# A Hymba-style block on one core: squares of x on two engines, parameter rows through GpSimd's queue, low parts of w_in on VectorE, scan parameters in steps

## The chip, the cores and the metric

One core of a Trainium2 chip runs the whole kernel. The metric is the device time of one execution in microseconds (us). The engines are named as in the profile: PE is TensorE, DVE VectorE, ACT ScalarE, POOL GpSimd, SP SyncE; each has an instruction queue of its own and takes its instructions in order.

## The reference

The input x has 1024 tokens of 1024 features, c is one conditioning vector. Cut to what matters here:

```python
c_act = jax.nn.silu(c)
mod = c_act @ ada_w + ada_b                  # shift, scale, gate, twice
h = modulate(rms_norm(x, norm1_g), sh1, sc1)
proj = h @ w_in                              # 1024 x (256 u, 3 x 512 q k v, 8 f, 3 x 256 conv)
u, q, k, v, f_logit, hc, bg, cg = split(proj)
y_ssm  = s5_mixer(u, ...)                    # complex scan over time, 16 groups of 64 states
y_attn = fox_attention(q, k, v, f_logit)     # rms_norm of q and k per head, forget gate, 8 heads of 64
y_conv = bg * conv3(cg * hc)
y = rms_norm(concat(y_ssm, y_attn, y_conv) per head) @ w_out
x = x + g1 * y
x = x + g2 * moe(modulate(rms_norm(x, norm2_g), sh2, sc2))   # 16 experts, top 2
```

In s5_mixer every state has `ab = exp(lam * dt)` (a magnitude `mag`, a sine and a cosine of `li * dt`); the kernel needs its first eight powers, the factor `z` of b, and the eighth power's phase.

## The kernel before

Matmuls of f32 data are done as three products of high and low parts: for a weight chunk in `feed` (L253) the high part is a copy by ACT into a rounded type (L280) and the low part a subtraction (`tt`, L95, called at L281). w_in comes in 40 chunks of 128x2x256; the first 8 low parts are on DVE, the 32 others on POOL. A projection group is 24 matmuls: high x high, low x high, high x low.

The order on every engine is the order in which the code is written. Four stretches concern the change.

**Start.** `load_x` (L156) issues x0 to x3 in turn from SP's and ACT's queues, SP then the ada_w blocks (`load_ada`, L308, the transfer at L314) and w_in chunks. ACT's queue further issues c_in (L202) and the five parameter rows into `prow` (L205, L207), then `Silu` of c (L216) and the four squares of the first half's tokens with their sums (`x_sq`, L432). The DMAs of SP and ACT share eight completion lanes, so a ninth waits until the first has landed. On PE `pvp` (L471) turns `prow`; DVE copies its parts out (L472 to L477), then makes the reciprocal root (`x_rs`, a chain from L123 over L110 to L115), scales x (L442), and PE turns it (`x_turn`, L447).

**The two loops over b (L536 and L972).** For half 0 and then half 1 of the tokens, each step turns x, makes h and its low part (`x_mod`: ACT L460, DVE L463 and L95) and multiplies with the conv channel hc (`groups`, L501). `sincos` (L370) and `s5_small` (L574), some 90 small DVE instructions on 128x8 to 128x32 elements that make the scan's parameters, stand behind the second loop.

**Conv and u groups.** `conv_group` for cg and bg and `u_group` (L951) are interleaved by `step`, one yield at a time, with generators: `s5_prep` (L622: products `ta`, `tb` with the powers on DVE, turns `pt` at L680, the kernel matrices `gk` by matmuls `pg` at L693 and L695), `s5_turns` (L707, complex powers on POOL in `tr` and `vroom`), and `conv_norm` (`pn`, L927). The result u goes to DRAM (`ud`) and comes back in another layout.

**q, k and v.** `project_steps` (L1026) makes a 128-token tile of q or k, ACT copies it (L1138) and squares it head by head (L1143), DVE copies the forget logits out (`f_sb`, L1140). `qk_norm` (L1040) puts the norm, the split and the turns into `later`, each for a beat counted in projections: QC, QD for q and KC, KD_ for k. `s5_main` (L779) is stepped between: once per projection until UG of them are done, twice after; its first yields lead to `px` (L796, the input of the scan, out of `ud`), then the two scans (L805, L807), `vv`, and `py` (L832).

Of the kernel before, what the change touches and what calls it, by code (L numbers as in the profile page):

```python
# [81 lines left out]
def _emit(tc, nc, V, A, G, T, I, out, dump, upto, stack):  # L82
# [386 lines left out]
    V.tensor_copy(cst[:, :, 0], c_act)  # L469
    pvp = ps_ms.tile([P, P], F32, name="pvp", tag="ms")  # L470
    T.transpose(pvp, prow, identF)  # L471
    V.tensor_copy(pv, pvp[:, :NPV])  # L472
    V.tensor_copy(lr, pvp[:, NPV:NPV + 8])
    V.tensor_copy(li, pvp[:, NPV + 8:NPV + 16])
    V.tensor_copy(dsk, pvp[0:16, NPV + 16:NPV + 32])
    for two in range(2):
        V.tensor_copy(ldt[64 * two:64 * two + 64, :], ldt16[64 * two:64 * two + 64, two:16:2])  # L477

# [1797 lines left out]
```

## Time and profile before

| what | us |
|---|---|
| median of 3 runs (lowest, highest) | 1109.03 (1107.26, 1115.13) |
| profiled execution | 1109.11 |
| its span, first to last instruction | 1107.4 |
| PE busy | 1008.4 (91%) |
| DVE busy | 719.8 (65%) |
| ACT busy | 523.5 (47%) |
| POOL busy | 291.9 (26%) |

The profile belongs to one execution. 1.7 us of its time lie around the span. The mean clock granted to TensorE over the span is 0.954 of full. A matmul's busy time is modelled, so the table's share says how rarely PE stands, not how well it is used. Times of rows count from the span's start.

### The profile page before, as it was taken

What the parts mean: (1) busy time and instruction counts of PE and PEld (TensorE: products, weight loads), DVE (VectorE), ACT (ScalarE), POOL (GpSimd) and SP (SyncE); (2) the same over time, 40 slices, a digit from 0 to 9 for tenths busy, and PEclk for the clock granted to TensorE, in tenths of its full rate; (3) what the DMA queues carried; (4) which work ended last, traced back from release to release, by engine and by line L of the source; (5) the groups of instructions that cost most, each with busy time, mean ns of one, the idle gap of its engine ahead of it and who ended that gap; (6) DMA issues with size and microseconds to landing.
All of it is one profiled execution on the core that took longest, in us unless ns stands there. A gap on an engine that the chain in (4) does not pass through costs nothing. (4 is left out here: it accounts for less than half of the span.)

```text
span 1107.4 us, 17980 instructions
## 1 busy us (share of the span) xinstructions
PE 1008.4 (91%) x6273; PEld 825.1 (75%) x6273; DVE 719.8 (65%) x1576; ACT 523.5 (47%) x1099; POOL 291.9 (26%) x312
## 2 busy tenths in 40 slices
PE   2999798899989998998899994999999999999995
PEld 1677578788778987887788883677777777777773
DVE  3679512926723344778466778895657899789593
ACT  3541113346444554777532222764435676567470
POOL 3006913233312002118312234112222212122121
PEclk9999789899989999999899995899999999999998
DMA  9701135015875444466255634896788699979772
GB/s 304 270 1 39 39 73 121 20 59 177 264 268 173 124 130 137 117 190 199 69 152 185 245 133 133 312 353 227 223 266 285 239 366 360 378 238 355 259 264 41
DMA packets 103006, 215.63 MB, mean 195 GB/s; under 512 B 14094, under 2 KB 37148, under 8 KB 102748
## 3 DMA queue, kind: packets, MB, share of 16 engines
q1 hardware_dynamic: 89744, 170.93, 46.0%
q0 software_dynamic: 12032, 40.60, 13.2%
q10 hardware_dynamic: 1116, 2.67, 0.7%
q8 instruction: 61, 1.00, 0.4%
q14 instruction: 53, 0.43, 0.1%
HBM read 185.47 MB, written 28.10 MB: 193 GB/s over the span
## 5 line engine op out<-in xcount | busy, mean ns | idle before, releaser
L95 DVE TENSOR_TENSOR wel<-wer,weh 128x1024 fp32r<-128x1024 f32 x192 | 223.1, 1216 | 2.9 <-ACT weh L1929 1.3
L1929 ACT ACTIVATE weh<-wer 128x1024 fp32r<-128x1024 f32 x192 | 188.9, 1053 | 5.0 <-ACTq L2185 1.7
L1984 POOL DMA_INDIRECT out_dram<-y,idx x28 | 56.9, 2033 | 234.2 <-DVE y L2049 139.4
L2012 PE MATMUL pg<-weh,xh 128*128 128x512 f32 x256 | 104.7, 409 | 2.0 <-ACT hid L2170 0.7
L2013 PE MATMUL pg<-weh,xl 128*128 128x512 f32 x256 | 103.1, 403 | 0.0
L95 DVE TENSOR_TENSOR pl<-ptp,ph 128x512 fp32r<-128x512 f32 (+1 forms) x80 | 50.3, 636 | 40.0 <-ACT ph L1321 39.7
L2017 PE MATMUL pg<-wel,xh 128*128 128x512 f32 x256 | 66.3, 397 | 0.0
L2012 PEld LDWEIGHTS pg<-weh,xh 128*128 128x128 f32 x256 | 49.1, 192 | 17.9 <-issue 6.1
L1321 ACT ACTIVATE ph<-ptp 128x512 fp32r<-128x512 f32 (+1 forms) x80 | 44.1, 553 | 31.3 <-PE ptp L1316 30.5
L2013 PEld LDWEIGHTS pg<-weh,xl 128*128 128x128 f32 x256 | 49.1, 192 | 11.6 <-DVE xl L95 0.4
L2017 PEld LDWEIGHTS pg<-wel,xh 128*128 128x128 f32 x256 | 47.7, 188 | 11.3
L1303 ACT ACTIVATE lg<-lg,mn 128x128 f32<-128x128 f32 (+3 forms) x64 | 49.5, 774 | 10.6 <-DVE mn L1292 10.6
L1316 PE MATMUL ptp<-identF,lg 128*128 128x128 f32 x288 | 48.1, 285 | 6.5 <-DVE pl L95 6.3
L2039 PE MATMUL pd<-weh,hh 128*128 128x512 f32 x128 | 52.2, 408 | 0.6 <-ACT hh L2031 0.5
L293 PE MATMUL pmw<-woh,yh 128*128 128x512 f32 x128 | 52.6, 411 | 0.0
L295 PE MATMUL pmw<-woh,yl 128*128 128x512 f32 x128 | 51.1, 399 | 0.0
L2040 PE MATMUL pd<-wel,hh 128*128 128x512 f32 x128 | 50.5, 395 | 0.0
L1336 PE MATMUL po<-ph,vs 128*128 128x256 f32 (+1 forms) x160 | 47.1, 315 | 1.2 <-ACT ot L1340 1.0
L1998 ACT ACTIVATE xh<-ptx 128x512 fp32r<-128x512 f32 x32 | 19.1, 598 | 60.9 <-issue 57.7
L1968 POOL DMA_INDIRECT xg<-h2d,idx x16 | 21.0, 1314 | 89.7 <-DVE wgt L1955 86.3
L1138 ACT ACTIVATE r<-pm 128x256 f32<-128x256 f32 x32 | 12.3, 384 | 61.7 <-PE pm L298 54.6
L1337 PE MATMUL po<-pl,vs 128*128 128x256 f32 (+1 forms) x160 | 40.3, 286 | 0.2
(658 smaller groups left out, 2679.1 us busy)
## 6 DMA issues: line engine op xcount, KB each, us to landing
wer<-in_w_up_dram SPq DMA_DIRECT2D x64, 512.0 KB, 8.6
wer<-in_w_gate_dram SPq DMA_DIRECT2D x63, 512.0 KB, 9.4
wer<-in_w_down_dram SPq DMA_DIRECT2D x63, 512.0 KB, 10.5
adw<-in_ada_w_dram SPq DMA_DIRECT2D x32, 512.0 KB, 4.9
vroom<-in_ada_w_dram SPq DMA_DIRECT2D x16, 512.0 KB, 8.7
xt<-in_x_dram SPq DMA_DIRECT2D x14, 512.0 KB, 7.1
qtd<-qe POOLq DMA_DIRECT2D x16, 256.0 KB, 4.2
qt<-qtd SPq DMA_DIRECT2D x16, 256.0 KB, 5.3
```

The costliest lines, as they stand in the source:

```text
L95: (eng or V).tensor_tensor(o, a, b, op=op)
L293: T.matmul(o, lhsT=sh(k), rhs=mh(k), start=(k == 0), stop=False)
L295: T.matmul(o, lhsT=sl(k), rhs=mh(k), start=False, stop=False)
L1303: A.activation(lg[:, :w], lg[:, :w], AF.Exp, bias=mn, scale=-1.0, accum_out=l_all[:, qb, h:h + 1])
L1316: T.transpose(pt[:, c0:c0 + P], lgs[u, b][0][:, k0:k0 + P], identF)
L1929: A.activation(hi, raw, AF.Copy)
L1984: G.indirect_dma_start(out=out[:, :], out_offset=bass.IndirectOffsetOnAxis(ap=ix, axis=0), in_=y, in_offset=None, compute_op=ALU.add)
L2012: T.matmul(pg, lhsT=x[0][:, k, :], rhs=hi, start=(k == 0), stop=False)
L2013: T.matmul(pg, lhsT=x[1][:, k, :], rhs=hi, start=False, stop=False)
L2017: T.matmul(pg, lhsT=x[0][:, k, :], rhs=lo, start=False, stop=(k == KD - 1))
L2039: T.matmul(pd, lhsT=h[0][:, k, :], rhs=hi[:, n, :], start=(k == 0), stop=False)
L2040: T.matmul(pd, lhsT=h[0][:, k, :], rhs=lo[:, n, :], start=False, stop=False)
```

## The change

Eight edits. (1) c_in's transfer comes first on ACT's queue and `Silu` right behind the x loads; the five parameter rows go to POOL's queue. (2) `load_bc`'s six transfers of ssm_b and ssm_c go from POOL's queue to SP's. (3) The squares of x1 and x3 are made by DVE in one instruction that multiplies and sums; ACT keeps x0 and x2. (4) `pvp` and the copies out of it stand behind the turns of half 0 instead of ahead of its norm. (5) All low parts of w_in are on DVE. (6) `sincos` and `s5_small` are one generator, of which steps are taken within the two loops over b. (7) Two yields more ahead of `gk` in `s5_prep`; UG 4 to 6, QD 5 to 6, KD_ 3 to 4. (8) q's factor is multiplied by DVE instead of POOL, and `f_sb` is copied by ACT instead of DVE.

```diff
-QC, QD, KC, KD_ = 3, 5, 2, 3
+QC, QD, KC, KD_ = 3, 6, 2, 4
-UG = 4
+UG = 6
...
+    c_in = cp.tile([P, 8], F32, name="c_in")
+    nc.scalar.dma_start(out=c_in, in_=I["c"].rearrange("o (p t) -> (o p) t", t=8))
     for i in range(4):
         load_x(i, nc.scalar if i % 2 else nc.sync)
+    c_act = cp.tile([P, 8], F32, name="c_act")
+    A.activation(c_act, c_in, AF.Silu)
...
-        nc.scalar.dma_start(out=prow[r0:r0 + n, :], in_=I[nm].rearrange("(r c) -> r c", c=P))
+        nc.gpsimd.dma_start(out=prow[r0:r0 + n, :], in_=I[nm].rearrange("(r c) -> r c", c=P))
...
-            tt(lo, raw[:, :, :m_], hi.bitcast(F32), ALU.subtract, V if at_w[1] <= 8 else G)
+            tt(lo, raw[:, :, :m_], hi.bitcast(F32), ALU.subtract)
...
-    def sincos(x):
+    def sincos(x, out):
...
+        yield
         cq = small()
...
         V.tensor_scalar(cq, cq, 1.0, None, op0=ALU.add)
+        yield
...
         V.tensor_scalar(pos, m, 1.0, None, op0=ALU.is_equal)
+        yield
...
         for j in js:
-            sq = st.tile([P, D], BF16, name="sqx", tag="sqx", bufs=1)
-            A.activation(sq, xts[half * 4 + j], AF.Square, accum_out=ss[:, j:j + 1])
+            x_ = xts[half * 4 + j]
+            if half == 0 and j % 2:
+                sq = st.tile([P, D], BF16, name="sqv", tag="sqv", bufs=1)
+                V.tensor_tensor_reduce(out=sq, in0=x_, in1=x_, scale=1.0, scalar=0.0, op0=ALU.mult, op1=ALU.add,
+                                       accum_out=ss[:, j:j + 1])
+            else:
...
             mag = vexp(mul(lr, dt_))
+            params = s5_small()
+        if b > 1:
+            next(params)
...
+        yield
+        yield
         gk = s5b.tile([16, 16, 8, 16], F32, name="gk", tag="wv")
...
                 x_mod(1, k)
+        for _ in range(2 if b < 4 else 1):
+            next(params, None)
         if b:
             groups(b - 1, "hc", 1)
-    th = mul(li, dt_)
-    sn, cs = sincos(th)
+    for _ in params:
+        pass
     es_st.close()
-    s5_small()
...
-                tt(r32, r32, gq[:, None, :].to_broadcast([P, 16, HD]), ALU.mult, G)
+                tt(r32, r32, gq[:, None, :].to_broadcast([P, 16, HD]), ALU.mult)
...
-                        V.tensor_copy(X["f_sb"][:, :, i4 * 4 + i], pm[:, 256:264])
+                        A.activation(X["f_sb"][:, :, i4 * 4 + i], pm[:, 256:264], AF.Copy)
```

`s5_small` has a yield behind each of its three rounds of powers, behind `z`, and behind each of the three squarings of the phase; its arithmetic is the same.

On ACT at the start, before, from the c_in transfer to the last square (`prow` are the parameter rows, `xt` x, `sqx` the squares; DMAHW0 to 7 are the completion lanes):

```order
L202 DMA c_in_109<-in_c_dram 128x8
L205 DMA prow_80<-in_ada_b_dram 48x128 [waits DVE_49]
L205 DMA prow_80<-in_norm1_g_dram 8x128 [waits DMAHW0_49]
L205 DMA prow_80<-in_norm2_g_dram 8x128 [waits DMAHW1_49]
L205 DMA prow_80<-in_out_norm_g_dram 8x128 [waits DMAHW3_49]
L207 DMA prow_80<-in_conv_w_dram 6x128 [waits DMAHW4_49]
L216 ACT_TABLE_LOAD
L216 ACTIVATE c_act_121<-c_in_109 128x8 [waits DMAHW5_49]
L432 ACTIVATE sqx_187,ssx_186<-xt_72 128x1024
L432 ACTIVATE sqx_189,ssx_186<-xt_74 128x1024 [waits Activation_49]
L432 ACTIVATE sqx_191,ssx_186<-xt_76 128x1024 [waits DMAHW2_49,Activation_49]
L432 ACTIVATE sqx_193,ssx_186<-xt_78 128x1024 [waits Activation_49]
```

and of the change, from the first instruction to the first low-part work:

```order
L162 DMA c_in_72<-in_c_dram 128x8
L158 DMA xt_76<-in_x_dram 128x1024
L158 DMA xt_80<-in_x_dram 128x1024
L166 ACT_TABLE_LOAD
L166 ACTIVATE c_act_82<-c_in_72 128x8 [waits DMAHW0_49]
L443 ACTIVATE sqx_178,ssx_177<-xt_74 128x1024 [waits DMAHW1_49]
L443 ACTIVATE sqx_182,ssx_177<-xt_78 128x1024 [waits DMAHW3_49,Activation_49]
L280 ACTIVATE wh__207<-hcs_152 128x2x256 [waits DMAHW5_49]
```

The five rows with their waits on lanes are gone ahead of `Silu`; two squares are left, and the high parts of w_in (`wh_`) follow them.

On DVE in the second loop over b, before, the last of half 1's casts and low parts (`hTh`, `hTl`) and the start of the parameters (`sm`):

```order
L463 CAST hTh_137<-h32_704 128x512 [waits Activation_49]
L95 TENSOR_TENSOR hTl_541<-h32_704,hTh_137 128x512 [waits DVE_49]
L463 CAST hTh_137<-h32_713 128x512 [waits Activation_49]
L95 TENSOR_TENSOR hTl_546<-h32_713,hTh_137 128x512 [waits DVE_49]
L95 TENSOR_TENSOR sm21_743<-sm3_170,sm13_316 128x8
L350 TENSOR_SCALAR sm22_745<-sm21_743 128x8 [waits DVE_49]
L351 TENSOR_SCALAR sm22_745<-sm22_745 128x8 [waits DVE_49]
```

and of the change, between the first two steps of that loop:

```order
L474 CAST hTh_137<-h32_662 128x512 [waits Activation_49]
L95 TENSOR_TENSOR hTl_270<-h32_662,hTh_137 128x512 [waits DVE_49]
L474 CAST hTh_137<-h32_671 128x512 [waits Activation_49]
L95 TENSOR_TENSOR hTl_275<-h32_671,hTh_137 128x512 [waits DVE_49]
L402 TENSOR_SCALAR sm33_675<-sm30_641 128x8
L95 TENSOR_TENSOR sm34_677<-sm25_494,sm33_675 128x8 [waits DVE_49]
L95 TENSOR_TENSOR sm35_679<-sm26_579,sm33_675 128x8
L95 TENSOR_TENSOR sm36_681<-sm26_579,sm30_641 128x8
L95 TENSOR_TENSOR sm34_677<-sm34_677,sm36_681 128x8 [waits DVE_49]
L95 TENSOR_TENSOR sm37_684<-sm25_494,sm30_641 128x8
L95 TENSOR_TENSOR sm35_679<-sm35_679,sm37_684 128x8 [waits DVE_49]
L95 TENSOR_TENSOR sm38_687<-sm32_643,sm31_642 128x8
```

The sine's last products (here the first of 24 instructions) now stand between the casts of step 0 and those of step 1.

On PE in the first u group, before (`pm` is the group, `wl__1004` the low parts of w_in's u chunk, `pt` the turns of `s5_prep`, `pg` the matmuls of `gk`):

```order
L680 MATMUL pt_1187<-identF_82,wbt_931 128x128 x3
L295 MATMUL pm_1173<-hTh_137,wl__1004 128x512
L293 MATMUL pm_1173<-hTh_137,wh__1003 128x512
L295 MATMUL pm_1173<-hTh_137,wl__1004 128x512 [waits Pool_49]
L293 MATMUL pm_1173<-hTh_137,wh__1003 128x512
L295 MATMUL pm_1173<-hTh_137,wl__1004 128x512
L293 MATMUL pm_1173<-hTh_137,wh__1003 128x512
L295 MATMUL pm_1173<-hTh_137,wl__1004 128x512 [waits Pool_49]
L693 MATMUL pg1_1201<-car_915,vroom_65 16x128 [waits DVE_49]
L695 MATMUL pg1_1201<-can_916,vroom_65 16x128 [waits DVE_49]
L693 MATMUL pg1_1201<-car_915,vroom_65 16x128
```

and of the change, the same place:

```order
L701 MATMUL pt_1187<-identF_86,wbt_931 128x128 x3
L295 MATMUL pm_1173<-hTh_137,wl__1004 128x512
L293 MATMUL pm_1173<-hTh_137,wh__1003 128x512
L295 MATMUL pm_1173<-hTh_137,wl__1004 128x512
L293 MATMUL pm_1173<-hTh_137,wh__1003 128x512
L295 MATMUL pm_1173<-hTh_137,wl__1004 128x512
L293 MATMUL pm_1173<-hTh_137,wh__1003 128x512
L295 MATMUL pm_1173<-hTh_137,wl__1004 128x512
L293 MATMUL pm_1173<-hTh_137,wh__1003 128x512
L295 MATMUL pm_1173<-hTh_137,wl__1004 128x512
L298 MATMUL pm_1173<-hTl_270,wh__1003 128x512
```

The low parts come without a wait on POOL, and the first `pg` matmuls stand ten places later, behind the whole group.

## Rows read from the trace of the kernel before

**Rows 1.** Stage 80 to 113.2 (busy us, instructions per engine, PE clock, DMA share)
```profile
80.00:113.20 33.20, 33.19 (x145) 26.43 (x143) 31.89 (x96) 4.15 (x9) 23.49 (x33) 1.00 0.13 33
```

**Rows 2.** Windows of the u and q stages, same columns
```profile
113.20:120.50 7.30, 4.43 (x26) 3.12 (x24) 7.27 (x5) 2.24 (x5) 7.14 (x6) 1.00 0.31 75
...
120.50:134.50 14.00, 9.44 (x30) 5.98 (x30) 4.75 (x6) 0.93 (x2) 13.61 (x15) 0.51 0.16 39
...
141.50:147.90 6.40, 6.40 (x21) 5.53 (x22) 0.00 (x0) 0.28 (x1) 0.00 (x0) 0.50 0.18 42
...
185.90:188.90 3.00, 3.00 (x20) 2.67 (x17) 1.66 (x5) 0.00 (x0) 0.00 (x0) 0.50 0.04 8
...
203.10:216.30 13.20, 10.61 (x62) 10.19 (x63) 11.16 (x14) 4.56 (x26) 1.72 (x1) 0.76 0.08 22
```

**Rows 3.** PE's waits from 0 to 400 (in total, times, longest)
```profile
PE pm L293 <- ACT sq L1143: 5.8, 3, 2.8
...
PE pm L295 <- POOL wl__1004 L95: 5.7, 2, 4.6
...
PE px L796 <- DMA vroom<-ud: 2.9, 1, 2.9
...
PE pt L680 <- ACT vroom L682: 1.7, 1, 1.7
```

**Rows 4.** ACT's timeline at the start (start, us, instruction)
```profile
5.75 0.83 ACTq L205 DMA_DIRECT2D prow<-in_norm_g_dram  x2
...
11.91 1.04 ACT L432 ACTIVATE sqx<-xt 128x1024 bf16<-128x1024 f32 x1
```

**Rows 5.** SP's timeline at the start
```profile
8.46 0.37 SPq L314 DMA_DIRECT2D vroom<-in_ada_w_dram  x1
```

**Rows 6.** DVE's timeline at the start
```profile
17.21 0.17 DVE L123 TENSOR_SCALAR rx_m<-ssx 128x4 f32<-128x4 f32 x1
```

**Rows 7.** Window 20 to 30, columns of rows 1
```profile
20.00:30.00 10.00, 8.89 (x56) 5.20 (x60) 5.40 (x13) 2.65 (x5) 0.00 (x0) 1.00 1.09 348
```

**Rows 8.** DVE's timeline around the scan parameters
```profile
75.79 0.69 DVE L95 TENSOR_TENSOR hTl<-h,hTh 128x512 fp32r<-128x512 f32 x1
...
83.33 1.16 DVE L95 TENSOR_TENSOR sm<-sm,sm 128x8 f32<-128x8 f32 x9
```

**Rows 9.** PE's timeline where the conv groups begin
```profile
79.22 0.40 PE L293 MATMUL pm<-hTh,wh__221 128*128 128x512 f32 x1
...
79.45 0.40 PE L295 MATMUL pm<-hTh,wl__222 128*128 128x512 f32 x1
```

**Rows 10.** POOL's timeline beside the u stage
```profile
111.67 2.48 POOL L95 TENSOR_TENSOR wl__1004<-wr__884,wh__1003 128x512 fp32r<-128x512 f32 x1
```

**Rows 11.** DVE's timeline at the same time
```profile
111.65 1.35 DVE L95 TENSOR_TENSOR ta<-vroom,sm 128x1152 f32<-128x1152 f32 x1
...
112.92 2.44 DVE L95 TENSOR_TENSOR tb<-vroom,sm 128x1152 f32<-128x1152 f32 x1
...
121.13 1.45 DVE L672 SCALAR_TENSOR_TENSOR can<-ta,tb 128x1152 f32<-128x1152 f32 x1
```

**Rows 12.** Waits of all engines, 168 to 264
```profile
ACT sq L1143 <- DVE f_sb L1140: 14.0, 8, 5.5
```

**Rows 13.** DVE's timeline in the q stage
```profile
182.95 0.17 DVE L1140 COPY f_sb<-pm 128x8 f32<-128x8 f32 x1 [2.75 <-ACT r L1138]
```

**Rows 14.** PE's timeline in the q stage
```profile
191.08 1.97 PE L796 MATMUL px<-vroom 128*64 128x128 f32 x32
```

**Rows 15.** DVE by line and form, 169 to 216 (busy, mean ns)
```profile
L805 DVE TENSOR_TENSOR_SCAN vroom<-vroom,vv 128x1024 f32<-128x1024 f32 x1 | 2.3, 2283 | 0.0
...
L95 DVE TENSOR_TENSOR t<-tr,vroom 128x1024 f32<-128x1024 f32 x1 | 2.1, 2129 | 0.0
...
L95 DVE TENSOR_TENSOR r<-r,rk_y 128x1024 f32<-128x1024 f32 x1 | 1.2, 1225 | 0.0
...
L95 DVE TENSOR_TENSOR t<-px,vroom 128x256 f32<-128x256 f32 x8 | 3.3, 418 | 0.1
```

More of the change, by code (lines that the diff above doesn't have):

```diff
@@ L408, in sincos @@
             tt(w_, w_, g_, ALU.mult)
-        return sw, cw
+        out.extend((sw, cw))
+        yield
     def cmul(o_re, o_im, ar, ai, br, bi, t1, t2, eng=None):
@@ L468, in _emit @@
     V.memset(cst, 0.0)
[L469 to L477, printed above, removed]
     def ada1(b):
@@ L526, in conv_out, with s5_small @@
             tt(hcs[:, cc, sl], pm, hcs[:, cc, sl], ALU.mult)
+    def s5_small():
+        out = []
+        yield from sincos(mul(li, dt_), out)
+        sn, cs = out
+        pwr, pwi = small((P, 9, 8)), small((P, 9, 8))
+        V.memset(pwr[:, 0, :], 1.0)
+        V.memset(pwi[:, 0, :], 0.0)
+        tt(pwr[:, 1, :], mag, cs, ALU.mult)
+        tt(pwi[:, 1, :], mag, sn, ALU.mult)
+        c1, c2 = small((P, 4, 8)), small((P, 4, 8))
+        for n in (1, 2, 4):
+            br = pwr[:, n:n + 1, :].to_broadcast([P, n, 8])
+            bi = pwi[:, n:n + 1, :].to_broadcast([P, n, 8])
+            cmul(pwr[:, n + 1:2 * n + 1, :], pwi[:, n + 1:2 * n + 1, :], pwr[:, 1:n + 1, :], pwi[:, 1:n + 1, :],
+                 br, bi, c1[:, :n], c2[:, :n])
+            yield
+        den = mul(lr, lr)
+        tt(den, den, mul(li, li), ALU.add)
+        V.reciprocal(den, den)
+        nre = small()
+        V.tensor_scalar(nre, pwr[:, 1, :], 1.0, None, op0=ALU.subtract)
+        zr, zi = mul(nre, lr), mul(pwi[:, 1, :], lr)
+        tt(zr, zr, mul(pwi[:, 1, :], li), ALU.add)
+        tt(zi, zi, mul(nre, li), ALU.subtract)
+        tt(zr, zr, den, ALU.mult)
+        tt(zi, zi, den, ALU.mult)
+        yield
+        m8, r, i = mag, cs, sn
+        for n in range(3):
+            m8 = mul(m8, m8)
+            nr, ni = mul(r, r), small()
+            V.scalar_tensor_tensor(ni, r, -2.0 if n == 2 else 2.0, i, op0=ALU.mult, op1=ALU.mult)
+            tt(nr, nr, mul(i, i), ALU.subtract)
+            r, i = nr, ni
+            yield
+        X.update(pwr=pwr, pwi=pwi, zr=zr, zi=zi, m8=m8, turn=(r, i))
     x_rms(0)
-    ada1p = st.tile([P, 8], F32, name="ada1p", bufs=1)
-    V.tensor_scalar(ada1p, adabT[:, 8:16], 1.0, None, op0=ALU.add)
+    V.tensor_copy(cst[:, :, 0], c_act)
     feed(2, 4)
@@ L535, in _emit @@
             ada1(0)
+    pvp = ps_ms.tile([P, P], F32, name="pvp", tag="ms")
+    T.transpose(pvp, prow, identF)
+    V.tensor_copy(pv, pvp[:, :NPV])
+    V.tensor_copy(lr, pvp[:, NPV:NPV + 8])
+    V.tensor_copy(li, pvp[:, NPV + 8:NPV + 16])
+    V.tensor_copy(dsk, pvp[0:16, NPV + 16:NPV + 32])
+    for two in range(2):
+        V.tensor_copy(ldt[64 * two:64 * two + 64, :], ldt16[64 * two:64 * two + 64, two:16:2])
+    ada1p = st.tile([P, 8], F32, name="ada1p", bufs=1)
+    V.tensor_scalar(ada1p, adabT[:, 8:16], 1.0, None, op0=ALU.add)
     for b in range(5):
@@ L683, in s5_prep @@
             yield
+        yield
+        yield
         gk = s5b.tile([16, 16, 8, 16], F32, name="gk", tag="wv")
```

42 lines of the change are left out of this document (5 added, 37 removed).

## The prediction

> **What bounds the kernel now.** I read the windows by stage first, then the waits of PE, then the timelines of the engines that PE waits for. In most stages PE stands at its work: from 80 to 113.2 it is busy 33.19 of 33.20 us [rows 1]. So I look for the stretches where it is not, or where it runs at the lower of its two clock levels (1.2 of 2.4 GHz, shown as 0.50). There are three. At the start nothing is multiplied until the first norm is ready, and DVE begins that norm at 17.21 [rows 6]. In the u stage the granted clock is 0.51 for 14 us and 0.50 for 6.4 us [rows 2], and ahead of and within these PE waits 5.7 us for low parts from POOL and 1.7 us for ACT [rows 3]. In the q stage PE waits 2.9 us for px's input and 5.8 us for ACT's squares [rows 3], again with half-rate stretches [rows 2]. ACT itself was held there by DVE's copy of the forget logits, 14.0 us in eight waits [rows 12]. No later stage is touched except the last turns of k, so I take a microsecond saved here as a microsecond of the whole. The profiled execution (1109.11) stands at the median of the runs (1109.03); I subtract from 1109.1.
>
> **A. The start.** ACT issues the first parameter rows at 5.75 and its four squares begin only at 11.91, each 1.04 and 0.15 for the sum, so they end near 16.6 [rows 4]. SP's ada_w transfer at 8.46 is the one that waits for x2's lane, so x2 has landed by then [rows 5]; x3, the second transfer of the same queue as x1, I put at 8.9. In the new order two squares are on ACT and two on DVE. A two-input DVE instruction of that size takes 1.23 [rows 15], so x3's ends at about 8.9 + 1.23 + 0.2 = 10.3 and the norm begins at 10.3 instead of 17.21: 6.9. Seven small copies out of pvp (0.8) now stand behind the turns and ahead of the sums that the modulation needs: 6.1 remain. What would be late next is ada_w: from 20 to 30 the transfers are at share 1.09 [rows 7], all engines full; by counting bytes at 348 GB/s each ada_w block lands 1 to 4 us ahead of its new time of need, so I let the whole gain stand. Bounds: 1 (the blocks arrive no sooner than PE wanted them) to 6.9. **+6.1.**
>
> ACT's five moved issues themselves take some 1.4 us (two of them 0.83 [rows 4]). The Trainium skill, "DMA: Bandwidth & Descriptors", section "Issuing engines are not separate DMA queues", says that starting transfers from several engines saves only the issuing time. By that rule the gain would be 1.4, not 6.1; the timeline speaks against it in so far as ACT stood behind waits for landings, not behind issues. It is rival 2.
>
> **B. The second loop.** Its DVE work gets the parameter steps. Their lengths come from the stretch after it: nine instructions of 128x8 take 1.16 there [rows 8], a dependent one about 0.2. Between the casts and low parts (0.43 and 0.69 each, the last at 75.79 [rows 8]) come 2.9 us in step 0, 2.0 in step 1, 2.3 in step 2 and 1.1 in step 3, and about 2.6 ahead of the loop. PE's own period is 3.7 us (a turn of 0.8 and 12 matmuls of 0.23, starts as in [rows 9]); DVE's becomes 2.2 + 2.9, 2.2 + 2.0, 2.2 + 2.3. The excess adds up to 3.7, and I let 1.5 of the 2.6 through: the conv groups begin at 79.22 + 5.2 if the start had gained nothing [rows 9]. Bounds: 0 (all hidden) and -10.9 (all in line). **-5.2.** In return DVE no longer has the 17 us behind the loop, which hid there beside PE's conv groups.
>
> **C. The u stage.** The waits of 5.7 for `wl` fall away, since DVE makes these parts at 0.69 and not POOL at 2.48 [rows 8, 10], and DVE is ahead: it is rid of the parameters at about 84 instead of 93.6 and takes some eight low parts (5.5) more before `can`, which ends at 122.5 before [rows 11]. That puts `can` at about 121 with the start's gain left out. PE would reach `gk` at 79.2 + 5.2 + 34.0 + 7.7 = 126.1 (24 matmuls of 0.23, 16 turns). So DVE leads by some 4 us, and the 1.7 for ACT goes too [rows 3]. With no gap in PE I expect no fall of the clock at 120.5: half of 9.44 is 4.7, half of 6.40 is 3.2 [rows 2]. With 2.6 of smaller gaps that is 5.7 + 1.7 + 4.7 + 3.2 + 2.6 = 17.9. Against that: the second fall came behind `gk`'s and the norm's small matmuls with hardly a wait, and these now lie closer together, so I keep 2.4 as lost there. Bounds: 0 (waits take another name) to 17.9. **+15.5.**
>
> **D. The q stage.** px is asked for two projections later, its data having had 2.9 us to miss; the squares no longer wait for DVE, ACT copying the logits itself; that is 2.9 + 5.8 + 0.7 for a turn, and half-rate stretches of 1.5 (3.00 at 0.50) and about 3.0 (13.2 at 0.76) [rows 2, 3], in all 13.9. New is this: `py` needs both parts of `vv`. PE reaches it after 13 projections of 2.93 (the copies of [rows 13] are 0.17 + 2.75 apart), 64 px matmuls (32 take 1.97 [rows 14]) and 16 turns, at 44.2 from q's first matmul. DVE gets px's last part after eight projections, at 27.4. It then has the products (six of 0.42), the split 1.2, a scan 2.28, the norm 2.5, two multiplications 2.45 (one of them taken over from POOL), a low part 0.7, the second scan 2.28, and two rounds of 2.13 + 1.2 + 1.2 [rows 15]: 27.4 + 2.5 + 20.5 = 50.4. PE stands 6.2 us, and I add 1.5 for a half-rate stretch behind it, as the one of 3.00 behind px's wait [rows 2]. 13.9 - 7.7 = **+6.2**. Bounds: -2 (the squares wait for something else) to 13.9.
>
> **E.** The last turns of k come one beat later, and what waits for them (attention's first scores) may be late by half a projection: **-1.0**, from -3 to +1. The six load_bc transfers on SP and the five on POOL I cost at nothing: they have tens of microseconds until `s5_prep`, and SP's queue has only blocks behind it that wait for buffers.
>
> Sum: 6.1 - 5.2 + 15.5 + 6.2 - 1.0 = 21.6; 1109.1 - 21.6 = 1087.5, say **1088**.
>
> **Rivals.** 1, slower: DVE becomes the bound. Beside POOL's 2.48 us low part, a DVE product of 128x1152 took 2.44, and the like one just ahead 1.35 [rows 10, 11]: 1.8 times. The chain of powers on POOL remains, and DVE's load between the loop and `gk` is 31.9 - 13.6 of moved parameters [rows 1] + 12.0 [rows 2] + 5.5 = 36 us. If all of it is stretched by 1.8, DVE is late by 36 x 0.8 - 4 = 25, and the half rate (7.9) comes back: 25 + 7.9 turn 21.6 into -11, **1120**. It decides from a stretch of 1.5. For it: the row; against it: POOL loses just the large instructions beside which DVE was slow.
>
> On this pair the Trainium skill, "GPSIMD Engine Reference", section "Key points", says that GpSimd shares its SBUF interfaces with VectorE, with contention where the DVE instruction has two SBUF inputs. All the moved low parts are such instructions; the rows agree that both engines were slow together, and no run here yet shows which kinds of POOL work do it.
>
> 2: the start is held by the transfers whoever issues them, A is 1.4: **1092**. For it the share of 1.09, against it that x2 and x3 have landed before 9.
>
> 3: the stalls and half rates form again elsewhere (behind the `gk` cluster, at `py`): C 8, D 2: 21.6 - 7.5 - 4.2 = 9.9, **1099**. For it: in this kernel nearly every gap of PE was followed by half rate.
>
> 4: `py` does not wait and the clock holds: 7.7 + 2.4 better, **1077**.
>
> **How the numbers follow.** The forecast has 0.43, with its own range of 1082 to 1094; rival 1 0.10, rival 2 0.13, rival 3 0.24, rival 4 0.10. One per cent, 11 us, is about what a measurement of this kernel can tell from no change: faster means below 1098, slower above 1120. A third of rival 3 (0.08) lies below 1098; with the forecast and rivals 2 and 4 that is 0.74 for faster. Of rival 1 I put 0.08 above 1120; 0.18 is left for the same. The range goes from 1074 to 1104: it leaves out rival 1 and the tails of 3 and 4.
>
> **What would show it.** Right: the first turn of x at about 13.5; the conv groups of cg begin at about 78; q's first matmul at about 153 (169.7 - 6.1 + 5.2 - 15.5); no wait of PE for `wl`; clock 1.00 from 110 to 125; px without a wait, py with one of about 6 us for DVE. Wrong: ada_w named as what PE waits for before 40, DVE's `ta`, `tb` at 2 us and more, PE waiting for DVE's low parts, or clock 0.50 in the u stage as long as before.

## The result, and the profile after

The changed kernel takes 1097.69 us (median of 20 runs, 1093.09 to 1109.22), the kernel before 1110.43 in 20 runs (1098.92 to 1115.78). The ratio of the compared runs is 0.9908, with an interval of 0.9883 to 0.9933. So the change is faster, clear of the noise, by 0.9% where 1.9% was forecast (21.6 of 1109.1). The prediction drew a line between faster and the same; the median, just below 1098, lies on one side of it and the ratio, just short of one per cent, on the other. The profiled execution took 1096.41, its span is 1094.7. Rival 3 (stalls and half rates form again elsewhere, 1099) is near what happened.

To see where the gain went I take the start of the same first instruction of each stage in both traces and subtract. A stage's own gain is the difference to the stage before. Both traces are of one execution; a second one of the changed kernel (e12 below) repeats every start up to k within 0.5 us.

| first instruction of | before | after | gain so far | own gain | forecast |
|---|---|---|---|---|---|
| half 0, turns of x | 20.41 | 14.02 | 6.4 | | |
| half 1, turns of x (A) | 63.18 | 57.55 | 5.6 | +5.6 | +6.1 |
| cg's conv group (B) | 79.22 | 77.52 | 1.7 | -3.9 | -5.2 |
| u stage, `pt` | 113.20 | 113.09 | 0.1 | -1.6 | |
| q's projections (C, from cg) | 169.72 | 162.28 | 7.4 | +7.3 | +15.5 (C) |
| k's projections (D) | 262.1 | 250.7 | 11.4 | +4.0, of the same work -1.4 | +6.2 |
| attention's first scores (E) | 365.7 | 354.6 | 11.1 | -0.3, of the same work +5.1 | -1.0 |
| end of the span | 1107.4 | 1094.7 | 12.7 | +1.6 | 0 |

A and B came near their terms, and C gave 7.3 - 1.6 = 5.7 of 15.5. D's 4.0 needs care: a stage's start is a fair mark only if the same work lies ahead of it. In the kernel before, 23 of the 32 matmuls `pgl` that follow the scan stand ahead of k; its PE groups by line, 169.7 to 262.1 (count, busy us, mean ns):

```profile
L862 PE MATMUL pgl<-vroom 128*128 128x256 f32 x23 | 5.4, 382 | 0.0
```

In after they all come behind k's first matmul, from 256.4 on:

```profile
L885 PE MATMUL pgl<-vroom x32: 377/379/451, 256.4 to 276.8; 128*128 128x256 f32 x32
```

So 5.4 us of work only changed sides: of the same work D is 4.0 - 5.4 = -1.4, and the stage behind it -0.3 + 5.4 = +5.1. The q stage, from which I expected 6.2, lost a little.

PE's waits of after, 0 to 400 (for whom, total, times, longest):

```profile
PE py L858 <- DVE vv L95: 3.2, 1, 3.2
...
PE py L856 <- DVE vv L95: 2.3, 1, 2.3
...
PE pa L484 <- DMA vroom<-in_ada_w_dram: 1.6, 1, 1.6
PE pm L514 <- DVE hTl L95: 1.6, 7, 0.2
PE pm L293 <- DVE hcs L95: 1.5, 1, 1.5
PE pg L718 <- DVE can L693: 1.4, 1, 1.4
...
PE pn L950 <- ACT zt L942: 0.8, 1, 0.8
```

The lines for `wl`, `sq`, `px` and the u stage's `pt` [rows 3] are gone, as forecast. In their place stand `py` (2.3 + 3.2, the forecast 6.2) and, not forecast, `hcs` and `can`: two products that DVE makes. The 0.8 for `zt` stood there before as well.

The windows of after, with the columns of [rows 2] (busy us and count of PE, PEld, DVE, ACT, POOL, then the granted clock):

```profile
77.60:113.00 35.40, 33.88 (x147) 26.84 (x146) 30.72 (x29) 5.59 (x10) 30.93 (x41) 1.00 0.18 45
113.00:125.50 12.50, 10.25 (x60) 7.58 (x57) 11.39 (x13) 4.48 (x9) 0.00 (x0) 1.00 0.19 45
125.50:136.50 11.00, 11.00 (x40) 8.81 (x41) 0.00 (x0) 1.49 (x3) 0.00 (x0) 0.53 0.11 25
136.50:146.00 9.50, 9.48 (x68) 7.21 (x67) 1.83 (x6) 2.89 (x5) 0.00 (x0) 1.00 0.20 63
146.00:150.00 4.00, 4.00 (x12) 3.13 (x11) 1.90 (x10) 0.00 (x0) 0.00 (x0) 0.57 0.55 99
...
211.00:232.00 21.00, 19.35 (x70) 15.89 (x70) 9.63 (x21) 4.30 (x14) 1.63 (x3) 0.51 0.20 62
```

In the u stage PE is still busy for 11.00 + 4.00 us at about half clock, where it was 9.44 + 6.40 before [rows 2]: the half rate has moved by 5 us and hardly shrunk. Its second stretch, from 146, came without a stand: from 125.5 PE is busy for 20.48 of 20.50 us, and what it did just before are 16 matmuls of two columns in a row (the conv norm, on PE's timeline):

```profile
143.56 1.95 PE L950 MATMUL pn<-blkF,zt 128*128 128x2 f32 x16
```

In the q stage there is one stretch of 21 us at 0.51, where there were 3.00 at 0.50 and 13.2 at 0.76 [rows 2]: twice as much half rate as before.

Why PE stands in the u stage is on DVE's timeline of after (start, us, instruction):

```profile
96.68 2.97 DVE L934 TENSOR_SCALAR hcs<-zt,pv 128x1024 f32<-128x1024 f32 x1
99.68 3.93 DVE L936 SCALAR_TENSOR_TENSOR hcs<-zt,pv,hcs 128x1024 f32<-128x1024 f32 x2
103.54 1.78 DVE L95 TENSOR_TENSOR wl__1004<-wr__884,wh__1003 128x512 fp32r<-128x512 f32 x1
...
106.69 0.68 DVE L95 TENSOR_TENSOR hcs<-pm,hcs 128x512 f32<-128x512 f32 x1
...
108.68 2.29 DVE L95 TENSOR_TENSOR tb<-vroom,sm 128x1024 f32<-128x1024 f32 x1
...
112.14 0.68 DVE L95 TENSOR_TENSOR wl__1004<-wr__941,wh__1003 128x512 fp32r<-128x512 f32 x1
...
121.13 1.36 DVE L693 SCALAR_TENSOR_TENSOR can<-ta,tb 128x1152 f32<-128x1152 f32 x1
```

A low part of the same size takes 1.78 at 103.54 and 0.68 at 112.14. In between POOL finished its chain of complex powers: it is busy 30.93 of 35.40 us up to 113, and 0.00 behind. The product that reads PSUM (`pm`) is not longer beside it: 0.68. And `can` begins at 121.13, to the hundredth where it began before [rows 11], with DVE busy without a pause from 83.3 on: what DVE was rid of in the parameters went into the low parts and into longer instructions beside POOL.

POOL's chain is the same in both kernels; its place is not. Some of its larger instructions, of after and then its first product of 128x256 of before:

```profile
88.82 1.49 POOL L95 TENSOR_TENSOR vroom<-tr 128x256 f32<-128x256 f32 x1
...
97.30 1.81 POOL L695 MEMSET kt<- 128x2048 f32 x1
99.06 1.48 POOL L95 TENSOR_TENSOR vroom<-tr 128x504 f32<-128x504 f32 x1
```

```profile
126.43 0.63 POOL L95 TENSOR_TENSOR vroom<-tr 128x256 f32<-128x256 f32 x1
```

The chain needs the scan's parameters. Edit 6 made these earlier, so the chain's first copy came at 76.40 instead of 93.76, and its large instructions, which before began behind `can`, now lay beside the conv taps and the products `ta` and `tb`. Before, the taps had only the chain's products up to 128x64 beside them, and the one that takes 2.97 above took 0.75.

The start, first ACT, then DVE:

```profile
5.09 1.04 ACT L443 ACTIVATE sqx<-xt 128x1024 bf16<-128x1024 f32 x1
...
7.17 1.06 ACT L443 ACTIVATE sqx<-xt 128x1024 bf16<-128x1024 f32 x1 [0.94 <-DMA xt<-in_x_dram]
```

```profile
9.40 1.22 DVE L439 CUSTOM_DVE_ANT_0 sqv<-xt 128x1024 bf16<-128x1024 f32 x1 [0.81 <-DMA xt<-in_x_dram]
...
10.74 0.17 DVE L123 TENSOR_SCALAR rx_m<-ssx 128x4 f32<-128x4 f32 x1
```

The norm begins at 10.74 (forecast 10.3) instead of 17.21 [rows 6]; no square stands behind parameter rows any more: x0's follows `Silu`, the others wait for their x.

### The profile page after: what moved, and what is told of

The parts are those of the page before. It is cut to its first block, busy times and chain, and to the rows that moved or that the text cites. A ratio compares the mean times of both kernels' runs of the same rounds, so it can differ in the third digit from the quotient of the medians.

```text
span 1094.7 us, 17976 instructions
## 1 busy us (share of the span) xinstructions
PE 1010.8 (92%) x6273; PEld 823.8 (75%) x6273; DVE 735.6 (67%) x1608; ACT 520.8 (48%) x1102; POOL 244.2 (22%) x275
## 5 line engine op out<-in xcount | busy, mean ns | idle before, releaser
L2008 POOL DMA_INDIRECT out_dram<-y,idx x28 | 64.2, 2293 | 221.1 <-DVE y L2073 136.3
L95 DVE TENSOR_TENSOR pl<-ptp,ph 128x512 fp32r<-128x512 f32 (+1 forms) x80 | 50.2, 635 | 38.9 <-ACT ph L1345 38.7
L2037 PEld LDWEIGHTS pg<-weh,xl 128*128 128x128 f32 x256 | 49.2, 192 | 11.5 <-DVE xl L95 0.4
```

The costliest lines, as they stand in the source:

```text
L95: (eng or V).tensor_tensor(o, a, b, op=op)
L2008: G.indirect_dma_start(out=out[:, :], out_offset=bass.IndirectOffsetOnAxis(ap=ix, axis=0), in_=y, in_offset=None, compute_op=ALU.add)
L2037: T.matmul(pg, lhsT=x[1][:, k, :], rhs=hi, start=False, stop=False)
```

## The experiments

Each is the kernel after with the edit shown, but the fourth, which is the kernel before with a part of the change. The starts of the stages on PE, and the times:

| | half 1 | cg | u | q | k | scores | median us | ratio, interval |
|---|---|---|---|---|---|---|---|---|
| before | 63.18 | 79.22 | 113.20 | 169.7 | 262.1 | 365.7 | 1110.43 | |
| after | 57.55 | 77.52 | 113.09 | 162.3 | 250.7 | 354.6 | 1097.69 | 0.9908, 0.9883-0.9933 |
| e1 | 57.84 | 77.84 | 113.42 | 162.3 | 246.1 | 353.2 | 1095.22 | 0.9878, 0.9813-0.9943 |
| e2 | 58.16 | 78.19 | 111.91 | 160.7 | 249.1 | 352.9 | 1095.91 | 0.9877, 0.9822-0.9933 |
| e3 | 57.78 | 77.81 | 111.53 | 162.5 | 251.5 | 356.2 | 1100.08 | 0.9915, 0.9882-0.9949 |
| e4 | 58.72 | 74.72 | 108.74 | 165.4 | 257.4 | 360.0 | 1099.19 | 0.9894, 0.9845-0.9943 |
| e5 | 57.35 | 77.33 | 112.94 | 152.8 | 247.5 | 352.4 | 1092.03 | 0.9873, 0.9808-0.9938 |
| e6 | 59.43 | 75.46 | 115.87 | 169.5 | 257.9 | 364.5 | 1100.29 | 0.9904, 0.9863-0.9945 |
| e7 | 59.68 | 79.67 | 115.25 | 173.2 | 258.8 | 363.9 | 1094.64 | 0.9885, 0.9816-0.9955 |
| e8 | 57.67 | 77.67 | 111.39 | 158.7 | 247.3 | 352.8 | 1095.18 | 0.9890, 0.9857-0.9923 |
| e9 | 59.48 | 79.49 | 113.21 | 158.4 | 247.0 | 351.2 | 1088.87 | 0.9815, 0.9784-0.9845 |
| e10 | 57.29 | 77.28 | 112.88 | 161.9 | 241.9 | 347.6 | 1087.64 | 0.9808, 0.9779-0.9838 |
| e11 | 57.89 | 77.89 | 111.62 | 153.7 | 233.6 | 342.3 | 1082.69 | 0.9767, 0.9741-0.9793 |
| e12 | 57.56 | 77.54 | 113.13 | 162.0 | 250.2 | 357.3 | 1098.11 | one run |

All intervals but those of e9, e10 and e11 overlap that of after. So for the steps I rely on the stages of the traces and not on the totals. The stages have a noise of their own: with the same start, half 1 begins between 57.3 and 58.2 in nine runs and between 59.4 and 59.7 in e6, e7 and e9. In these three the clock was at its lower level from about 26.5 to 30.5, behind a wait of 1.9 us for ada_w; behind the same wait it did not fall in e1, e5 and e12. Differences of 2 us that begin there are not read. In e1, e10 and e11 a further 12 turns of the scan's result (some 1.9 us) stand behind k's start that in after are ahead of it; their k is compared with 1.9 added. Theory and rival are named anew in each expectation.

**e1: no wait at `py`.** The scan's outputs are asked for four steps later.

```diff
-PY = 5
+PY = 9
```

> The changed kernel with py two projections of q later (PY 5 to 9), so that PE reaches py about 50 us after q's first matmul, when DVE is done with vv. Theory 1 (the 20 us at half rate follow the 5.5 us for which PE stands at py): no wait at py, clock 1.00 through py, k's first matmul at about 236 instead of 250.7, the whole some 13 to 15 us below the changed kernel, near 1083. Rival (py's thin matmuls bring the half rate themselves): only the wait goes, 3 to 5 us. Rival (the time comes back where py's results are needed): within 2 us of the changed kernel.

`py` does not wait, q's start is the same, k's is 4.6 us earlier, 2.7 for the same work. But PE stands 10.1 us at another place, and half clock is still there, from 213.9 to 224.9, for 5 us of it with PE at work. `py`'s own matmuls, which now find their data, run at full clock. PE's waits, and then ACT's, 180 to 250:

```profile
PE pm L293 <- ACT sq L1167: 10.5, 2, 10.1
```

```profile
ACT r L1162 <- DVE rk_m L123: 12.6, 1, 12.6
```

ACT's copy `r` of a tile of q finds both its buffers held, since DVE's norm and split of q stand in line behind the scan's products. DVE's work between px and the end of `vv` is the limit; a later `py` only moves the place at which PE meets it.

**e2: POOL's powers later, by program order.** The generator `s5_turns` is stepped with the u groups, from ahead of the first, instead of beside cg.

```diff
-            if (nm, cc) == ("cg", 0):
-                side2.append(s5_turns())
...
+    side4 = [s5_turns()]
...
+        step(2, side4)
```

> The changed kernel with POOL's chain of powers begun with the u stage instead of behind the first conv group. Theory 1 (DVE is slow between 86 and 113 because POOL works beside it): the conv taps, 2.97 and 1.97 us there, go back to 0.75 to 1.36, the products tb from 2.29 to about 1.3, PE's waits of 1.5 us for hcs and 1.4 us for can go, DVE is 5 us and more ahead at gk; the whole 3 to 5 us below the changed kernel if the half rate behind gk stays, 9 to 11 if it goes with the waits. Rival (DVE is slow there for a reason of its own): the durations stay and so does the time.

A miss as an experiment: nothing on POOL stands ahead of the chain and its inputs were ready, so it began at 78 all the same: a later place in the program alone did not hold it back. The test was mended as e8. One thing it separates, though. On POOL the memset of `kt`, which is part of `s5_prep`, came ahead of the chain, at 76.13, instead of within it. DVE's timeline of e2:

```profile
96.11 1.11 DVE L934 TENSOR_SCALAR hcs<-zt,pv 128x1024 f32<-128x1024 f32 x1
```

The tap that took 2.97 beside this memset takes 1.11 beside the chain's products of 128x256. `can` is done 1.2 us earlier, and the u stage begins 1.2 us earlier.

**e3: the low parts on POOL again.**

```diff
-            tt(lo, raw[:, :, :m_], hi.bitcast(F32), ALU.subtract)
+            tt(lo, raw[:, :, :m_], hi.bitcast(F32), ALU.subtract, V if at_w[1] <= 8 else G)
```

> The changed kernel with the low parts of w_in behind the eighth back on POOL. Theory 1 (this edit bought the u stage's 7 us): PE waits for POOL's low parts again, 4 to 7 us in the u stage, and the half rate is longer; the whole 5 to 9 us above the changed kernel. Rival (the low parts on DVE cost as much there, by stretching DVE, as they saved): within 2 us.

The u stage begins 1.6 us earlier, without the wait for `hcs`, then PE waits 1.5 us for `wl` and 1.4 for `pt`; q begins at 162.5 against 162.3. The move of the low parts, on which 5.7 us of my sum stood, is worth nothing that shows in the changed kernel.

**e4: the start alone.** Edits 1, 3 and 4 on the kernel before.

```diff
+    nc.scalar.dma_start(out=c_in, in_=I["c"].rearrange("o (p t) -> (o p) t", t=8))
...
+    A.activation(c_act, c_in, AF.Silu)
...
-        nc.scalar.dma_start(out=prow[r0:r0 + n, :], in_=I[nm].rearrange("(r c) -> r c", c=P))
+        nc.gpsimd.dma_start(out=prow[r0:r0 + n, :], in_=I[nm].rearrange("(r c) -> r c", c=P))
...
+            if half == 0 and j % 2:
...
+                V.tensor_tensor_reduce(out=sq, in0=x_, in1=x_, scale=1.0, scalar=0.0, op0=ALU.mult, op1=ALU.add,
```

> The kernel before with the start alone changed: c_in first, parameter rows on POOL's queue, two squares on DVE, pvp behind the turns. Theory 1 (the start's gain of 5.6 us passes through to the end): first turn at about 14, the second loop begins near 57.5, the whole 5 to 6 us below the kernel before. Rival (the low parts from POOL and the u and q data come no sooner, so later waits grow by what the start saved): 0 to 2 us below.

Half 1 begins 4.5 us earlier and the gain stays: 4.3 at q, 4.7 at k, 5.7 at the scores. So the start is about half of the whole gain (11.1 at the scores). The transfers took back 1.8: the first turn comes 6.3 us earlier (14.16), then PE waits 2.0 for ada_w. That much is rival 2, and no more. By the total (0.9894) it can't be told from the whole change.

**e5: no wait in the u stage.** Two yields more ahead of `gk`, and one more in the conv norm.

```diff
+        yield
+        yield
...
+        yield
```

> The changed kernel with two more yields ahead of gk and one more in the conv norm ahead of its first matmuls, so that PE finds can and zt done. Theory 1 (the half rate from 125 to 136 follows PE's stands of 1.4 and 0.8 us just ahead of it): no wait of PE for can or zt, clock 1.00 from 120 to 136, q's first matmul 6 to 9 us earlier (near 154 to 156). Rival (the thin matmuls of gk and of the norm bring it, waits or not): the waits of 2.2 go, the half rate stays at 10 us, q's first matmul near 160.

The whole u stage of e5 in one window, then its waits 80 to 270:

```profile
112.94:152.80 39.86, 39.81 (x274) 31.97 (x272) 18.03 (x33) 10.99 (x20) 0.00 (x0) 1.00 0.24 55
```

```profile
PE pm L293 <- ACT sq L1170: 4.7, 1, 4.7
PE py L860 <- DVE vv L95: 2.9, 1, 2.9
PE py L858 <- DVE vv L95: 2.4, 1, 2.4
PE pm L293 <- DVE hcs L95: 1.5, 1, 1.5
```

Without a stand in the u stage the clock is 1.00 throughout, and the 273 matmuls that take 49.2 us in after take 39.9. q begins at 152.8; I had forecast 153. Two things limit the reading. The 1.5 us for `hcs` stand ahead of the stage, at 106, and no fall followed them, here or in after. And the added yields also spread the thin matmuls: the 16 of `pn` that after has in a row come one pair at a time. But the later conv norm delays the store `cd`, for which ACT's copies of q wait 11.9 us, so PE stands 4.7 and runs at half clock from 162.5 to 169.7: of 9.5 us 3.2 are left at k.

**e6: the parameters in one piece.** No steps within the loops.

```diff
-        if b > 1:
-            next(params)
...
-        for _ in range(2 if b < 4 else 1):
-            next(params, None)
```

> The changed kernel with the scan's parameters made in one piece behind the second loop, as before. Theory 1 (the steps cost 3.9 us in the loop and bring DVE ahead in the u stage): the conv groups begin at 73.6 instead of 77.5; PE then waits for DVE's low parts and for can, the u stage is 5 to 9 us longer, the whole 1 to 5 us above the changed kernel. Rival (the steps only cost): the 3.9 us pass through, the whole 3 to 4 us below.

The second loop takes 16.0 us as before instead of 20.0, so the steps cost 3.9. Given back at once: PE waits 4.2 us for a low part of w_in, the clock is 0.50 from 91.3 to 98.1, and the u stage begins 2.8 us later than in after (1.9 of it from the start). The total (0.9904) doesn't tell the steps' worth: six of ten runs took 1100 to 1104 us, four 1091 to 1093, and the profiled one, of the six, ran 28 us at half clock in the u stage (129 to 157) with one stand of 0.8 ahead of it.

**e7: UG 4 with the later `py`.**

```diff
-PY = 5
-UG = 6
+PY = 9
+UG = 4
```

> The changed kernel with px two projections of q earlier (UG 6 to 4) and py where it is (PY 5 to 9), so that DVE has 5.9 us more for the scan between them. Theory 1 (DVE is late at py by 5.5 us, and the half rate follows that stand): px waits 0 to 2 us for its data, py waits for nothing or under 1 us, clock 1.00 from 205 to 230, k's first matmul near 236 to 240 instead of 250.7; the whole 11 to 15 us below the changed kernel. Rival (DVE has too much work in the stage wherever px stands): ACT or PE waits for DVE elsewhere and k begins within 3 us of 250.7.

PE stands 4.4 us ahead of `px`, which the waits put down to issue; POOL issued the transfers of u out of `ud` from 177.2 to 181.7 and `px` came at 190.3, so I read it as the wait of 2.9 before [rows 3]. It stands 3.1 for `sq`. From q to k it takes 85.6 us against 88.4 in after, but e1, which differs from it in UG alone, takes 83.8 + 1.9 = 85.7: what the earlier `px` wins at the end it loses ahead of itself. Whether the later `px` of the change is needed is not shown. This execution, the slowest of four (1102.5; the fastest 1091.7), ran 34 us at half clock in the u stage, of which below.

**e8: POOL's chain held back in fact.** As e2, but the chain's steps begin behind the first u group, and its first two copies are made by DVE there, so that POOL has to wait for them.

```diff
-            G.tensor_copy(o_[:, :, 1], e_)
+            V.tensor_copy(o_[:, :, 1], e_)
```

> The changed kernel with POOL's chain of powers held back: its first two copies are DVE's and stand behind the first u group, so POOL begins at about 124 instead of 76. (In the run before, POOL only waited for its own inputs and began at 78 all the same.) Theory 1 (DVE is slow from 86 to 113 since POOL works beside it): the conv taps of 2.97 and 3.93 us go to 0.75 and 2.6, tb from 2.29 to 1.3, no wait of 1.5 us at 107, DVE is done with can 4 us and more earlier; u begins at 111.5; q's first matmul 2 to 3 us earlier with the half rate as it is, 8 to 10 if it goes. Rival (DVE is slow there from its own operands): the durations stay.

DVE's timeline of e8, the instructions shown above of after:

```profile
94.27 0.75 DVE L934 TENSOR_SCALAR hcs<-zt,pv 128x1024 f32<-128x1024 f32 x1
95.06 2.61 DVE L936 SCALAR_TENSOR_TENSOR hcs<-zt,pv,hcs 128x1024 f32<-128x1024 f32 x2
97.58 0.68 DVE L95 TENSOR_TENSOR wl__976<-wr__884,wh__975 128x512 fp32r<-128x512 f32 x1
...
98.78 0.68 DVE L95 TENSOR_TENSOR hcs<-pm,hcs 128x512 f32<-128x512 f32 x1
...
100.52 1.22 DVE L95 TENSOR_TENSOR tb<-vroom,sm 128x1024 f32<-128x1024 f32 x1
...
111.90 1.36 DVE L693 SCALAR_TENSOR_TENSOR can<-ta,tb 128x1152 f32<-128x1152 f32 x1
```

With POOL silent from 78 to 120.9 `can` begins 9.2 us earlier, and the waits for `hcs` and `can` are gone. That is my rival 1 at a small scale, shown. But a half-rate stretch of 10 us remains (122 to 132.5), behind the wait of 0.8 for `zt` in the conv norm, and one of 4 us (142 to 146) behind the 16 `pn` in a row, without a wait; q is 3.6 us earlier, not 9.

**e9: e8, and the conv norm's small matmuls later.** Six empty places ahead of `pn`, so that its input is ready.

```diff
+            else:
+                smalls.extend([lambda: None] * 6)
```

> The run with POOL's powers held back, and the conv norm's first matmuls six matmuls later, so that PE finds both can and zt done. Theory 1 (the half rate in the u stage follows PE's stands): no wait in the u stage, clock 1.00 from 110 to 150, q's first matmul near 152; and since the norm's last step is not pushed to the end of the stage, q's squares do not wait. k's first matmul near 240. Rival (half rate comes with the thin matmuls, and the run with the added yields lost it because it spread them): half rate for 10 us as in the run with POOL held, q near 158.

```profile
122.00:135.50 13.50, 12.82 (x85) 9.89 (x84) 2.48 (x5) 4.97 (x9) 11.01 (x34) 1.00 0.20 61
135.50:146.50 11.00, 11.00 (x42) 9.04 (x40) 5.39 (x13) 0.59 (x1) 8.24 (x9) 0.53 0.48 70
146.50:158.40 11.90, 11.90 (x100) 9.49 (x98) 3.20 (x7) 2.25 (x4) 0.00 (x0) 1.00 0.29 87
```

The first fall is gone; another, of 10 us, comes behind the only wait that is left, 0.7 us, at a cluster of `pg` (64 rows) and `pn` (two columns). The u stage takes 45.2 us against 49.2. So the stand need not be long, and the second stretches of after and e8 had none at all. Nor do thin matmuls bring it each time: before had the same 16 `pn` in a row at 152.7, at full clock throughout. What decides it these runs do not separate.

**e10: the q stage relieved on both sides.** `py` later, and q's split and turns asked for one projection earlier.

```diff
-QC, QD, KC, KD_ = 3, 6, 2, 4
+QC, QD, KC, KD_ = 2, 5, 2, 4
...
-PY = 5
+PY = 9
```

> The changed kernel with py two projections later (PY 5 to 9) and q's split and turns one beat earlier (QC 3 to 2, QD 6 to 5), so that DVE's split of q's second block is not queued behind the whole of vv. Theory 1 (with py late, ACT's buffer of q waited for that split, and PE for ACT, 10 us): PE waits for ACT's squares under 4 us, for py under 3 us, the half rate from 216 to 224 shrinks; k's first matmul near 238 to 242. Rival (DVE has no room in this stage, whichever instruction stands first): PE stands 8 to 10 us somewhere between 205 and 220, k's first matmul stays at 246.

ACT's squares wait 0.3 us instead of e1's 10.1, PE meets DVE once, 5.9 us at `ptk`, and half rate lasts 7 us (213.7 to 220.5) instead of 20.5. k begins 6.9 us earlier than in after for the same work (241.9 + 1.9 against 250.7).

**e11: e9 and e10 together.**

```diff
-QC, QD, KC, KD_ = 3, 6, 2, 4
+QC, QD, KC, KD_ = 2, 5, 2, 4
...
-PY = 5
+PY = 9
...
-            G.tensor_copy(o_[:, :, 1], e_)
+            V.tensor_copy(o_[:, :, 1], e_)
...
+            else:
+                smalls.extend([lambda: None] * 6)
```

> The last two together. If the two gains add: q's first matmul near 152, k's near 228 to 232, the whole 15 to 20 us below the changed kernel, near 1078 to 1083. If the q stage gives back what the u stage saves (px waits for u's way through DRAM, which takes some 18 us from the last u group), k near 236 to 240 and the whole 8 to 12 us below.

```profile
136.50:140.50 4.00, 4.00 (x14) 3.25 (x14) 3.68 (x8) 0.00 (x0) 3.84 (x5) 0.57 0.19 22
140.50:153.60 13.10, 13.10 (x104) 10.48 (x102) 5.94 (x12) 2.26 (x4) 2.16 (x2) 1.00 0.55 109
```

The rest of its u stage from its only fall on. q begins at 153.7 and k at 233.6 + 1.9, 15.2 us earlier than in after, where e9 and e10 had 3.7 and 6.9; the scores come 12.3 earlier. The gains do more than add up to k, and that is chance: e9 began half 1 1.9 us later than after did, e11 0.3, and the fall lasted 4 us here and 10 in e9. A part is given back ahead of the scores, where PE waits 6.6 us for ada_w's rows instead of 2.4. At 1082.69 us (0.9767) it beats both kernels, with an interval clear of after's.

**e12: the kernel after again.**

> The changed kernel once more, word for word. If the length of the half rate in the u stage is set by the order of the work: 10 to 11 us again, from 125. If it differs from execution to execution, as 11 us in the changed kernel and 33 us in the run with the scan earlier (whose u stage has the same instructions) suggest: another length.

Up to k every stage begins within 0.5 us of the first profile, with half clock in the same places (124.9 to 135.1, 145.3 to 148.6); the scores are 2.7 us later. e7 has the same u stage but there:

```profile
126.00:160.00 34.00, 33.48 (x117) 24.13 (x116) 4.44 (x16) 5.55 (x10) 0.00 (x0) 0.50 0.18 41
```

and after in the same window:

```profile
126.00:160.00 34.00, 33.98 (x180) 26.66 (x180) 5.63 (x18) 5.01 (x9) 0.00 (x0) 0.80 0.32 72
```

The same instructions behind the same waits (1.5, 1.4, and 0.5 for 0.8) ran 34 us at the lower level there and about 14 here. Why the stretch is longer in one execution stays open. It is no small matter: it sets 10 us of the time, as much as the change itself.

## Why the prediction was wrong, point by point

**Direction and A, right.** Start 5.6 of 6.1. The squares were held by ACT's line of waiting transfers, and e4 shows that the gain reaches the scores (5.7). How it divides over the edits 1, 3 and 4 no run separates. 1.6 us of waiting for ada_w did appear, so rival 2 was at work: the first group gained 4.1 (31.3 to 27.19) where the first turn had gained 6.4, but at half 1 it is 5.6 again.

**B, right.** 3.9 of 5.2, and e6 gives the 3.9 by itself. The excesses that the prediction lists, 1.4, 0.5 and 0.8, add up to 2.7 and not to 3.7; its own steps give 4.2.

**C, the failed step.** "So DVE leads by some 4 us" and, from it, "With no gap in PE I expect no fall of the clock". The slack counted the moved low parts and the removed parameters at their undisturbed durations, though [rows 10, 11] had shown DVE longer beside POOL. I put this away as rival 1 because "POOL loses just the large instructions beside which DVE was slow". It lost those of w_in, but edit 6 moved the chain of powers, with products of up to 128x504 and a memset of 128x2048, from behind `can` to beside the work that leads to it. `can` was to be done 36.6 us behind the start of the conv groups (121 - 84.4); in after it was done 45.0 us behind it, in e8, where the chain is held back, 35.6. So DVE's work was costed rightly but for POOL, and PE stood 1.5 + 1.4 us for it; the 0.8 for `zt`, which the sum counted as going, stayed. The ratio of 1.8 was misread too: `ta`, the "like one just ahead" at 111.65, lay beside the same low part of POOL (111.67 to 114.15) and was not longer, so not every instruction is. And from the terms given (122.5 - 9.6 + 5.5) `can` comes at 118.4, not 121, a longer lead than the one that failed.

In numbers: before, PE was idle 8.2 us in the u stage; my 5.7 + 1.7 + 2.6 = 10.0 held 1.8 us that did not exist, since the smaller gaps were little more than one of 0.8. After, 2.3 are idle there and 1.5 ahead of it. That makes 8.2 - 3.8 = 4.4 instead of 10.0. For half rate I had put 7.9 - 2.4 = 5.5; it gave 1.4 (busy 48.3 us before, 46.9 after, for the same 273 matmuls). 4.4 + 1.4 is 5.8, the 5.7 of the table. e8 and e5 show the two parts: without POOL beside DVE the waits for `hcs` and `can` go, and q gains 3.6; with no stand and the thin matmuls spread the clock stays, and q begins at the time that I forecast. That the clock stays wherever PE has no gap is not shown: after's second fall came without one. The 2.4 kept as lost for it was near (3.4 us at half rate, 1.7).

On this pair the Trainium skill, "GPSIMD Engine Reference", section "Key points", says that there is contention for DVE instructions with two SBUF inputs or in a two-port mode. The rows agree as to the kinds: two SBUF inputs 0.68 to 1.78 and 1.22 to 2.29, an input from PSUM 0.68 in both. The one-input `TENSOR_SCALAR`, 0.75 to 2.97 (1.11 in e2), is not of the first kind; whether it is of the second no row says. I had quoted the rule for the low parts alone and charged it to none of the terms.

**D, the second failed step.** The times on DVE held: `vv` was ready 50.2 us behind q's first matmul (forecast 50.4), PE reached `py` at 44.0 (44.2), stood 2.3 + 3.2 = 5.5 (6.2), and the waits for `px` and `sq` went. What failed is "1.5 for a half-rate stretch behind it": the stretch lasted some 20 us (211.1 to 231.6, and within 0.2 us as long in e5 and e12). `py`'s matmuls show it on PE's timeline of after (start, us, and the wait ahead in brackets):

```profile
206.28 0.38 PE L855 MATMUL py<-kt,vroom 128*128 128x128 f32 x2
209.00 0.49 PE L856 MATMUL py<-car,vv 64*128 64x128 f32 x2 [2.34 <-DVE vv L95]
212.65 0.79 PE L858 MATMUL py<-can,vv 64*128 64x128 f32 x2 [3.16 <-DVE vv L95]
213.37 0.79 PE L855 MATMUL py<-kt,vroom 128*128 128x128 f32 x2
```

The pair that takes 0.38 ahead of the waits takes 0.79 behind them. In numbers: PE's idle time from q to k fell from 9.5 to 6.9 us, 2.6 of the forecast 3.2 (9.4 of waits gone, 6.2 new). Its busy time for the same work rose from 82.9 to 81.6 + 5.4 = 87.0, that is -4.1 where I had put 4.5 - 1.5 = +3.0. 2.6 - 4.1 is the -1.5 of the table but for rounding. e10 shows the stage without the two waits in a row: 6.9 us better. `py`'s matmuls are not the cause by themselves, since in e1 they ran at full clock; why this stretch is six times as long as those of the kernel before in this stage (3.0 to 3.4 us each) stays open.

**E, wrong and on the good side.** +5.1 of the same work instead of -1.0. "No later stage is touched" overlooked PE's waits for ada_w's second rows. They stand between k and the scores, first of before, then of after:

```profile
PE pr L1100 <- DMA adw<-in_ada_w_dram: 6.3, 3, 3.7
```

```profile
PE pr L1124 <- DMA adw<-in_ada_w_dram: 2.4, 3, 1.1
```

That is 3.9 us, and a half-rate stretch that before had from 312 to 319 is not in after. How much of this the change did is open: e12, the same kernel, waited 3.8 there and had such a stretch from 333 to 336.5, and over all runs this wait is between 1.1 and 6.6. Of the 1.6 us behind the scores I name no cause either.

**The rivals.** 1 happened in kind and at a fraction of its size; 3 in its result, at the two places that it named (`gk` and `py`), with 5.7 and -1.4 where it had 8 and 2, and 5.1 behind them that no case had. Giving it 0.24 and the forecast 0.43 was the wrong way round: the forecast needed every stand in the u stage to vanish. That the total came out near 1098 is in part luck: 5.1 + 1.6 of its 12.7 us are stages that the forecast held untouched, and without them it would have been near 1104.

## What to carry to other kernels

A gain that consists of "the clock will not fall" does not shrink in step with the stands: e8 took away the two that it was meant to and kept two stretches of half clock of 10 and 4 us, e5 had none left in that stage. Give such a gain a chance of its own, and expect it to differ between executions of one kernel (14 and 34 us of half clock here). When work is moved onto an engine, cost it at the durations that the engine shows beside what the other engines do then, not at its quiet ones. When work is made earlier, ask what it releases: here the parameters released POOL's chain, which then lay beside DVE's work. And look at what the moved wait uncovers on the engine behind it: e1, e5 and e7 each removed one wait and met the next.
